# A two-block network in one emission-scheduled kernel: new TensorE estimates in the planner and an explicit wait in the norm

## The chip, the cores and the metric

The kernel runs on one core of a Trainium2 chip. The metric is the device time of one launch in microseconds. It is the median of three runs, which lay within 0.4 us of each other, and one more execution was profiled. Times inside the program (starts, waits, durations) are those of that profiled execution.

## What is computed

The input is 512 tokens of width 1024 in f32. Two blocks of two layers each run one after the other. Cut to what matters, with the first block's token mixers and the loop around them:

```python
def _token_mixers(h, ...):
    a_val, a_gate, q_att, k_att, v_att, q_rec, z_fwd, z_bwd, i_rec, g_rec = split(h @ w_in)
    a = depthwise_conv(a_val * sigmoid(a_gate), conv_w, conv_b)         # 31 taps, 256 channels
    a = silu(layernorm(a))
    att = mixture_of_dilated_attention(q_att, k_att, v_att)             # 6 heads, 3 dilations
    o_r = hgrn2_scan(forward) + hgrn2_scan(backward)                    # 6 heads, gated linear scan
    rec = rmsnorm_per_head(o_r) * rec_norm_w * silu(g_rec)
    return concatenate([a, att, rec]) @ w_out

def first_block(x, ...):
    for l in range(2):
        h = rmsnorm(x) * (1 + sc1) + sh1
        x = x + g1 * _token_mixers(h, ...)
        h = rmsnorm(x) * (1 + sc2) + sh2
        x = x + g2 * ((gelu(conv3(h @ w_up)[gate]) * conv3(h @ w_up)[val]) @ w_down)
    return rmsnorm(x)
```

The second block's layers project in the same way to three attentions (one that keeps the 128 best keys of each query, one over a sliding window with sinks, one of stick-breaking form), mix them with gates and add the result to x.

## The kernel before

**Tiling.** x lies transposed in SBUF, as eight tiles of 128 channels by 512 tokens. A projection is a row of *slots*: a slot is one 128-column piece of a weight matrix times the whole input, that is eight steps over k (`k_step`), each of three matmuls, because a f32 product is made of two rounded halves: high by high, low by high, high by low (`hh,hi`, `hl,hi`, `hh,lo` in the rows). A slot so has 24 matmuls of 128x512, accumulates in one of two PSUM banks called `proj`, and ends with its `consume`, which empties the bank on ScalarE (ACT) or VectorE (DVE). The weights are split into halves on those two engines (`hi<-raw` mostly on ACT, `lo<-raw,hi` on DVE), and an accumulation over the modulation's weights (`ada`) runs on DVE.

**Streams and the planner.** All else, the attentions, the scan, the convolution's norm, the top-k, is written as Python generators, *streams*. While the program is built, the class `Kernel` keeps an estimated clock of TensorE (`self.clock`) and of the other engines (`self.t`), with a cost for each instruction: `charge` for DVE and ACT, `pe` for TensorE. After each `k_step`, `products` lets up to four stream steps (NPUMP) be emitted, of those whose estimated due time has come (`pump`). So the estimates set no instruction and no wait: they decide only between which slot matmuls a stream's instructions stand. Each engine then runs its instructions strictly in that order, and waits by semaphores for what it reads. `bank` lets a stream take a `tr` or `sc` bank of PSUM (two of each) once its readers are estimated to be done.

**The convolution.** Its 31 taps for two channel tiles are 62 multiply-adds on DVE (`conv_taps`). They are emitted where DVE is estimated to be idle for over 0.6 us (FILL, in `charge`), and as a slow stream where DVE's estimated backlog is under 1 us. When all taps are out, the stream `conv_norm` follows: transposes of four into a bank, statistics and scaling on DVE, a square root and a sigmoid on ACT (each needs its own table load), transposes back.

**The order of block 1's mixer.** `block1_layer` lists the slots as `r0 a t0 t1 r1 r2 t2 g P`: scan pair 0, the convolution's inputs, attention pairs 0 and 1, and so on, the scan's three gates (`g`), and then the first half of the output projection (`P`). In layer 0 these are slots 0 to 27 for the inputs and 28 to 31 for `P`. The first of `P` multiplies what the convolution and attention pairs 0 and 1 have left in `mx`, and so has a step ahead of it: `drain("conv","conv","att0","att1")` emits stream steps, of whichever streams are due, until none of those three is alive. While it runs, no slot's matmul is emitted.

**Turn-overs.** Between passes that depend on a norm, the last slots of a pass (the tail) run in halves of 256 tokens, `half_norm` makes the new normalised tiles `hh` and `hl` for each half, and the slots behind wait for those tiles. Weight halves of some tail slots are kept in `hh` and `hl` themselves (`in_h`), until these slots' matmuls are through.

The rows below name PSUM and SBUF tiles: `proj`, `tr`, `sc`, `pva`, `pvs` are banks, `arena` and `stay` are working buffers, `mx` holds mixer outputs, `sm` small statistics, `colt` per-channel constants. A wrapper issues all DVE and ACT work, so that its line is always L113. L346 is the matmul in `mm`, L350 the transpose in `tp`.

Of the kernel before, what the change touches and what calls it, by code (L numbers as in the profile page):

```python
# [116 lines left out]
class Slot:  # L117


    def __init__(self, src, nk, rhs, consume=None, start=True, stop=True, pre=None, name="", parts=None):  # L120
        self.name = name
        self.ada, self.tail = 0, 0
        self.own, self.lead, self.place = None, False, None
# [69 lines left out]
class Kernel:  # L193
# [4 lines left out]
    def __init__(self, ctx, tc, ins, out, cfg):  # L198
# [15 lines left out]
        self.clock = 0.0  # L214
        self.streams = []
# [123 lines left out]
    def pe(self, out, reads, cost):  # L339
        start, rk, wk = self.begin("P", reads, [out])  # L340
        start = max(start, self.clock)
        self.clock = start + cost
        self.end("P", self.clock, rk, wk)

    def mm(self, out, lhsT, rhs, start, stop, cost):
        self.nc.tensor.matmul(out, lhsT, rhs, start=start, stop=stop)  # L346
        self.pe(out, (lhsT, rhs), cost)

    def tp(self, out, in_):
        self.nc.tensor.transpose(out, in_, self.ident)  # L350
        self.pe(out, (in_,), 0.122)
# [188 lines left out]
    def start_up(self):  # L540
# [7 lines left out]
        for _ in range(WARM):  # L548
            self.mm(warm, self.sq2[:, 0:P], self.sq2, True, True, 1.6)
# [46 lines left out]
        for n in range(KT):  # L596
# [16 lines left out]
            for j, (d, p) in enumerate(zip(duo, accs)):  # L613
                self.mm(p, d.raw[:, n * P:(n + 1) * P], self.hraw[n].ap, n == 0, n == KT - 1, 0.858)
# [194 lines left out]
    def k_step(self, s, p, kt, start, stop, c=ALL):  # L809
# [3 lines left out]
        cost = 0.216 if c == ALL else 0.109  # L813
        self.mm(p[:, c], wh, hh, start, False, cost)
        self.mm(p[:, c], wh, hl, False, False, cost)
        self.mm(p[:, c], wl, hh, False, stop, cost)
# [52 lines left out]
    def turn_over(self, i, k):  # L869
# [11 lines left out]
        self.made = [0, 0]  # L881
        for s in tail:
# [75 lines left out]
    def bias_mm(self, bb, duo, kt, only=None):  # L958

        for j, d in enumerate(duo):  # L960
            if only in (None, d):
                self.mm(bb[:, j:j + 1], d.raw[:, kt * P:(kt + 1) * P], self.nB[:, kt:kt + 1], j == 0 and kt == 0,
                        j == len(duo) - 1 and kt == KT - 1, 0.214)
# [86 lines left out]
    def norm_stream(self):  # L1050
# [3 lines left out]
        if st is None:  # L1054
# [3 lines left out]
            for q, sq in enumerate((self.sq, self.sq2)[:1 + fin]):  # L1058
                for j in range(4):
                    self.mm(st[:, 4 * q + j:4 * q + j + 1], sq[:, j * P:(j + 1) * P], self.ones[:, 0:1], True, True, 0.22)  # L1060
# [16 lines left out]
        for b in bufs:  # L1077
            rb = yield from self.bank("tr")
            for j in range(4):
                self.mm(rb[:, j * P:(j + 1) * P], b.ap[:, j * P:(j + 1) * P], self.ident, True, True, 0.226)  # L1080
# [3 lines left out]
    def half_norm(self, hf, c, outs, me, after):  # L1084
# [5 lines left out]
        for q, sq in enumerate(sqs):  # L1090
            for j in range(2):
                self.mm(st[:, 2 * q + j:2 * q + j + 1], sq[:, j * P:(j + 1) * P], self.ones[:, 0:1], True, True, 0.22)
# [13 lines left out]
        for b in bufs:  # L1106
# [3 lines left out]
            for j in range(2):  # L1110
                self.mm(rb[:, j * P:(j + 1) * P], b[:, j * P:(j + 1) * P], self.ident, True, True, 0.226)
# [10 lines left out]
        for n in range(KT + 1):  # L1122
            if n < KT:
                t = self.tmps[n % 2].ap[:, c]
# [43 lines left out]
    def two(self, outs, lhsT, rhs, start, stop, n, k0=0):  # L1168

        for hh in range(2):  # L1170
            self.mm(outs[hh], lhsT[hh], rhs[hh], start, stop, 0.06 if hh == 0 else max(0.858 * n / S, 0.06))

    def pv_add(self, pv, V, j, o, n, rhs, start, stop):

        self.two([pv[64 * h:64 * h + 64, o:o + n] for h in range(2)], [V[:, j, 64 * h:64 * h + 64] for h in range(2)],
                 rhs, start, stop, n)

    def attend(self, heads, span, stride, size, score, V, vo, tag, done, extra=0):
# [9 lines left out]
        for qt in range(5):  # L1188
            if qt < 4:
# [7 lines left out]
                for hh in range(2):  # L1197
                    rows = slice(64 * hh, 64 * hh + 64)
                    self.mm(scs[hh][:, 0:n], q.ap[rows, qt * P:(qt + 1) * P], k.ap[rows, kt0 * P:kt0 * P + n],
                            True, not extra, 0.858 * n / S)  # L1200
# [31 lines left out]
        for kt in (0, 2, 1, 3):  # L1232
# [3 lines left out]
                     [x[:, a:a + n] for x in pts], kt == 0, kt == 3, n)  # L1236
# [104 lines left out]
    def scan_stream(self, l, p, q, T0b, Kb, vbox, gbox, out):  # L1341
# [12 lines left out]
        def scores(w, lhsT, rhs, cost):  # L1354
# [3 lines left out]
            for j in range(4):  # L1358
                for b in range(P // w):
                    k0 = j * P + b * w  # L1360
                    for hh, rows in enumerate(heads):
                        self.mm(scs[hh][b * w:b * w + w, j * w:j * w + w], lhsT[rows, k0:k0 + w], rhs(j, b)[rows],
                                True, True, cost)
# [5 lines left out]
        scs = yield from scores(32, ks.ap, lambda j, b: q.ap[:, j * P + 32 * b:j * P + 32 * b + 32], 0.036)  # L1369
# [9 lines left out]
        for lev in range(7):  # L1379
# [20 lines left out]
            scs = yield from scores(w, km.ap, rhs, 0.036 if w == 32 else 0.083)  # L1400
# [37 lines left out]
        for d in range(2):  # L1438
            for e in range(3):
                i, j = 3 * d + e, 3 - e if d else e  # L1440
                for hh in range(2):
                    self.mm(kv[64 * hh:64 * hh + 64, i * 64:i * 64 + 64],
                            ktb.ap[:, d * S + e * P + 64 * hh:d * S + e * P + 64 * hh + 64],
                            V[:, j, 64 * hh:64 * hh + 64], True, True, 0.083)
# [16 lines left out]
        for e in range(3):  # L1461
            for d in range(2):
                i, j = 3 * d + e, 2 - e if d else e + 1
                c = slice((1 - d) * S + j * P, (1 - d) * S + (j + 1) * P)
                for hh, rows in enumerate(heads):
                    self.mm(pv[rows, j * P:(j + 1) * P], st[rows, i * 64:i * 64 + 64], Q[rows, c], False, e == 2 and d == 1, 0.136)
# [10 lines left out]
        for j in range(4):  # L1477
            self.mm(st[:, 2 * j:2 * j + 2], sq.ap[:, j * P:(j + 1) * P], self.bones, True, True, 0.22)
# [5 lines left out]
        for j in range(4):  # L1484
            self.mm(rb[:, j * P:(j + 1) * P], sq.ap[:, j * P:(j + 1) * P], self.ident, True, True, 0.226)
# [838 lines left out]
```

## Time and profile before

| | us |
|---|---|
| median of 3 runs | 2585.87 (2585.79 to 2586.15) |
| the profiled execution's own time | 2588.26 |
| its span | 2586.5 |
| TensorE busy in the span | 2538.2 (98%), 15404 matmul passes |
| DVE busy | 1773.5 (69%) |
| ACT busy | 1339.2 (52%) |

The profiled execution is 2.39 us above the median, and 1.76 us of its time lie outside the span. To read it: the page's first part tells how little TensorE idles, the waits tell for whom, the windows tell where the other engines are full and where TensorE's clock was lowered, and the timeline of each engine shows the single places.

### The profile page before, as it was taken

How to read it: one execution, taken by the hardware profiler on the slowest of the kernel's cores; microseconds unless marked ns; L12 is line 12 of the kernel's file. 1: busy time of each engine (PE TensorE's matmuls, PEld its weight loads, DVE VectorE, ACT ScalarE, POOL GpSimd, SP SyncE). 2: the span in 40 equal slices, each digit the busy share in tenths (PEclk: the TensorE clock that was granted, in tenths of full speed). 3: DMA queues.
4: the chain of work that ended last, by engine and by line, in shares of the span. 5: the costliest groups of instructions: out<-in, count | busy, mean ns of one | idle time of the engine just before them, and what ended most of it. 6: DMA issues, size and time to landing. Idle time of an engine off the chain costs nothing.

```text
span 2586.5 us, 39181 instructions
## 1 busy us (share of the span) xinstructions
PE 2538.2 (98%) x15404; PEld 1995.5 (77%) x15404; DVE 1773.5 (69%) x3368; ACT 1339.2 (52%) x2345; POOL 0.2 (0%) x4
## 2 busy tenths in 40 slices
PE   9999999999999999999999999999999999999998
PEld 5767788888977768888897677777779667777787
DVE  7897687655689767665667896556556697546645
ACT  4686554323457664442345446666435455666622
POOL 0000000000000000000000000000000000000000
PEclk9999999999999999999999999999999999999999
DMA  7433324444333222443442222223342112222222
GB/s 260 138 136 118 123 99 154 147 147 150 111 137 112 90 106 82 139 141 136 131 139 82 74 77 99 102 94 104 109 129 95 58 70 78 90 78 90 86 90 90
DMA packets 90071, 290.32 MB, mean 112 GB/s; under 512 B 10016, under 2 KB 13728, under 8 KB 89888
## 3 DMA queue, kind: packets, MB, share of 16 engines
q1 hardware_dynamic: 87728, 281.76, 32.1%
q10 hardware_dynamic: 2160, 6.06, 0.7%
q8 instruction: 122, 2.00, 0.3%
q14 instruction: 61, 0.50, 0.1%
HBM read 285.69 MB, written 2.10 MB: 111 GB/s over the span
## 4 chain that ended last, share of the span: by engine, by line
PE 82%; DVE 10%; ACT 4%; DMA 2%; issue 1%; SPq 0%; ACTq 0%; DVEq 0%
PE proj L346 68%; PE sc L346 7%; DVE arena L113 6%; PE tr L350 3%; PE pva L346 3%; ACT arena L113 3%; DVE lo L113 1%; PE pvs L346 1%; ACT L113 1%; DVE sm L113 1%; PE tr L346 1%; DVE hl L113 1%; DVE ada L113 0%; ACT hi L113 0%; DMA arena<-w_in 0%
## 5 line engine op out<-in xcount | busy, mean ns | idle before, releaser
L346 PE MATMUL proj<-hh,hi 128*128 128x512 f32 (+1 forms) x2232 | 896.9, 402 | 7.0 <-DVE arena L113 2.6
L346 PE MATMUL proj<-hl,hi 128*128 128x512 f32 (+1 forms) x2232 | 869.7, 390 | 5.3 <-DVE hl L113 5.3
L346 PE MATMUL proj<-hh,lo 128*128 128x512 f32 (+1 forms) x2232 | 869.8, 390 | 0.5 <-DVE lo L113 0.5
L346 PEld LDWEIGHTS proj<-hh,hi 128*128 128x128 f32 x2232 | 420.2, 188 | 138.3 <-issue 43.9
L113 DVE TENSOR_TENSOR lo<-raw,hi 128x1024 fp32r<-128x1024 f32 (+2 forms) x381 | 436.0, 1144 | 99.4 <-ACT hi L113 95.6
L346 PEld LDWEIGHTS proj<-hh,lo 128*128 128x128 f32 x2232 | 419.9, 188 | 90.3 <-DVE lo L113 1.0
L346 PEld LDWEIGHTS proj<-hl,hi 128*128 128x128 f32 x2232 | 420.7, 188 | 85.4 <-DVE hl L113 8.5
L113 ACT CAST hi<-raw 128x1024 fp32r<-128x1024 f32 (+2 forms) x340 | 333.7, 982 | 100.8 <-PE proj L346 63.6
L346 PE MATMUL proj<-rar,hi 128*128 128x512 f32 x672 | 208.9, 392 | 0.0
L113 DVE SCALAR_TENSOR_TENSOR arena<-proj,colt,arena 128x511 f32<-128x511 f32 x164 | 122.9, 749 | 103.8 <-ACT arena L113 100.9
L113 DVE TENSOR_TENSOR arena<-arena 128x512 f32<-128x512 f32 (+8 forms) x321 | 173.0, 558 | 25.7 <-ACT arena L113 18.8
L113 ACT ACT_TABLE_LOAD x134 | 171.9, 1283 | 17.7 <-DVE sm L113 8.6
L113 ACT COPY arena<-tr 128x512 f32<-128x512 f32 (+3 forms) x266 | 111.2, 458 | 115.3 <-PE tr L350 105.2
L113 DVE SCALAR_TENSOR_TENSOR ada<-ada,cbc 128x1024 f32<-128x1024 f32 x128 | 155.8, 1217 | 0.2 <-DMA ada<-ada 0.2
L346 PEld LDWEIGHTS proj<-rar,hi 128*128 128x128 f32 x672 | 124.9, 188 | 29.7 <-issue 4.6
L346 PE MATMUL sc<-arena 64*32 64x32 f32 (+6 forms) x3024 | 143.8, 248 | 3.5 <-issue 3.1
L113 ACT ACTIVATE arena<-proj 128x512 f32<-128x512 f32 x113 | 66.8, 599 | 155.1 <-PE proj L346 147.4
L113 ACT ACTIVATE arena<-proj,colt 128x512 f32<-128x512 f32 x82 | 56.4, 687 | 170.7 <-PE proj L346 168.5
L346 PE MATMUL proj<-mx,hi 128*128 128x512 f32 x432 | 136.3, 397 | 2.5 <-DVE x L113 2.5
L113 ACT ACTIVATE arena<-arena,sm 128x512 f32<-128x512 f32 (+3 forms) x180 | 105.1, 585 | 59.8 <-DVE sm L113 58.9
L113 DVE SCALAR_TENSOR_TENSOR x<-proj,mod,x 128x512 f32<-128x512 f32 (+1 forms) x102 | 64.6, 634 | 103.8 <-PE proj L346 102.9
L346 PE MATMUL proj<-rar,lo 128*128 128x512 f32 x336 | 130.9, 390 | 0.0
(219 smaller groups left out, 3082.4 us busy)
## 6 DMA issues: line engine op xcount, KB each, us to landing
raw<-w_in SPq DMA_DIRECT2D x190, 512.0 KB, 3.3
ada<-ada SPq DMA_DIRECT2D x128, 512.0 KB, 4.6
raw<-w_up SPq DMA_DIRECT2D x88, 512.0 KB, 3.3
raw<-w_out SPq DMA_DIRECT2D x32, 512.0 KB, 3.4
raw<-w_down SPq DMA_DIRECT2D x32, 512.0 KB, 3.6
raw<-w_br SPq DMA_DIRECT2D x48, 256.0 KB, 2.6
arena<-ada SPq DMA_DIRECT2D x16, 512.0 KB, 7.3
raw<-w_down SPq DMA_DIRECT2D x16, 384.0 KB, 3.2
```

The source lines that it names most:

```text
L113: return f(*a, **kw)
L346: self.nc.tensor.matmul(out, lhsT, rhs, start=start, stop=stop)
L350: self.nc.tensor.transpose(out, in_, self.ident)
```

## The change

Only numbers that set the order change, and one wait in the planning of `half_norm`. The instructions are the same ones.

- `pe` and `mm` no longer take a cost from the caller. `mm` works it out from type, split of the array and width: a 128x512 slot matmul goes from 0.216 to 0.2272 us and a 256-wide one from 0.109 to 0.1205; a pair of 64-row score matmuls (two heads) from 1.716 to 0.877 us; a 32x32 matmul of the scan from 0.036 to 0.022; a transpose from 0.122 to 0.109.
- `self.mode` remembers the split of the array that the last matmul used. A matmul with another split is charged 0.1 us more when it leaves the full array and 0.2 us more otherwise.
- The four warm-up matmuls of each block add 0.74 us each to the clock, beside their new cost.
- `half_norm` now waits, in the planner, while a tile that it is about to write still holds the weight halves of a tail slot whose matmuls are not all emitted (`s.hi is not None`).

```diff
-    def pe(self, out, reads, cost):
+    def pe(self, out, reads, cost, mode):
         start, rk, wk = self.begin("P", reads, [out])
         start = max(start, self.clock)
+        if mode != self.mode:
+            cost += 0.1 if self.mode == (128, 128) else 0.2
+            self.mode = mode
         self.clock = start + cost
         self.end("P", self.clock, rk, wk)

-    def mm(self, out, lhsT, rhs, start, stop, cost):
+    def mm(self, out, lhsT, rhs, start, stop):
         self.nc.tensor.matmul(out, lhsT, rhs, start=start, stop=stop)
-        self.pe(out, (lhsT, rhs), cost)
+        rows, cols, n = lhsT.ap[0][1], lhsT.free_size(), rhs.free_size()
+        mode = tuple(32 if x <= 32 else 64 if x <= 64 else 128 for x in (rows, cols))
+        if lhsT.dtype == F32R:
+            cost = 0.0137 + n * 0.000417
+        elif lhsT.dtype == BF16:
+            cost = 0.0137 + max(n, 64) * 0.000417
+        elif mode == (128, 128):
+            cost = 0.015 + max(n, 128) * 0.00167
+        elif n <= 32:
+            cost = 0.022
+        else:
+            cost = 0.01 + n * 0.000837
+        self.pe(out, (lhsT, rhs), cost, mode)

     def tp(self, out, in_):
         self.nc.tensor.transpose(out, in_, self.ident)
-        self.pe(out, (in_,), 0.122)
+        self.pe(out, (in_,), 0.109, (128, 128))
...
-        cost = 0.216 if c == ALL else 0.109
-        self.mm(p[:, c], wh, hh, start, False, cost)
+        self.mm(p[:, c], wh, hh, start, False)
...
+        self.in_tail = tail
         for s in tail:
...
         for n in range(KT + 1):
             if n < KT:
+                while any(n in s.h_tiles and s.hi is not None for s in self.in_tail):
+                    yield (self.clock + 0.1,)
                 t = self.tmps[n % 2].ap[:, c]
```

**The place between the last gate and the output projection, block 1, layer 0, TensorE.** Before, the end of slot 27 (`proj_2664`) and the first of `P` (`proj_2776<-mx`), with the scan's `pvs`, the attention's `tr` and `sc` between them:

```order
L346 MATMUL proj_2664<-hh,hi_2403 128x512
L346 MATMUL proj_2664<-hl,hi_2403 128x512
L346 MATMUL proj_2664<-hh,lo_2404 128x512
L346 MATMUL proj_2776<-mx,hi_2535 128x512 x2
L346 MATMUL proj_2776<-mx,lo_2536 128x512
L350 MATMUL tr_2780<-ident,arena_89 128x128 x4
L350 MATMUL tr_2786<-ident,arena_89 128x128 x4
L346 MATMUL pvs_2754<-arena_89 64x128 x12
L346 MATMUL sc_2806<-arena_89 128x512
L346 MATMUL sc_2807<-arena_89 128x512
L346 MATMUL proj_2776<-mx,hi_2535 128x512 x2
L346 MATMUL proj_2776<-mx,lo_2536 128x512
```

Now the same place begins with the last matmul of slot 27 (`proj_2676`):

```order
L352 MATMUL proj_2676<-hh,lo_2427 128x512
L368 MATMUL tr_2743<-ident,arena_89 128x128 x4
L368 MATMUL tr_2751<-ident,arena_89 128x128 x4
L352 MATMUL sc_2757<-arena_89 128x512
L352 MATMUL sc_2758<-arena_89 128x512
L352 MATMUL tr_2765<-ident,arena_89 128x128 x4
L368 MATMUL tr_2777<-ident,arena_89 128x128 x4
L368 MATMUL tr_2783<-ident,arena_89 128x128 x4
L368 MATMUL tr_2789<-ident,arena_89 128x128 x4
L352 MATMUL sc_2795<-arena_89 128x512
L352 MATMUL sc_2796<-arena_89 128x512
L368 MATMUL tr_2826<-ident,arena_89 128x128 x4
```

Five more groups of four transposes and the eight rows of `pva` follow before the first matmul on `mx`: the drain stood inside the slots' matmuls before, with `P` running between its parts, and stands now as one piece of 60 stream matmuls and transposes with nothing of a slot in it. Of these, 44 belong to attention pair 2, 12 to the convolution's norm and 4 to the scan.

**The same place on ACT, now.** The rows are part of what the drain emits: the attention's softmax (`arena,sm`), copies out of `tr`, the table loads, and the convolution's square root (`sm_2819<-sm_2806,eps`) and first sigmoid (`arena<-tr_2841,colt`):

```order
L113 COPY stay<-tr_2789 128x4x128
L113 ACTIVATE arena_89,sm_2608<-arena_89,sm_2607 128x512 x2
L113 ACTIVATE arena_89<-arena_89,sm_2608 128x512
L113 ACT_TABLE_LOAD
L113 ACTIVATE sm_2819<-sm_2806,eps 128x4
L113 COPY arena_89<-tr_2826 128x4x128
L113 COPY stay<-tr_2832 128x4x128
L113 ACTIVATE arena_89<-arena_89,sm_2608 128x512
L113 ACT_TABLE_LOAD
L113 ACTIVATE arena_89<-tr_2841,colt 128x512 x2
L113 CAST mx<-arena_89 128x512
L113 COPY arena_89<-tr_2851 128x4x128
```

Before, the convolution's two sigmoids and both its `CAST mx` stood on ACT ahead of the evacuations of the last two gates. Now they stand inside the drain: the second `CAST mx` is the third row below those shown.

**Layer 1, the convolution's norm and the scan of pair 1, TensorE.** Before, four transposes of the convolution (`tr_8161`) stood directly ahead of a scan level's 32 score matmuls (`sc_8171`, `sc_8172`, of which the first two stand here) and its transposes:

```order
L350 MATMUL tr_8161<-ident,arena_5966 128x128 x4
L346 MATMUL sc_8171<-stay,arena_5966 64x64
L346 MATMUL sc_8172<-stay,arena_5966 64x64
...
L350 MATMUL tr_8198<-ident,arena_5966 128x128 x3
L350 MATMUL tr_8203<-ident,arena_5966 128x128 x3
L346 MATMUL proj_8217<-hh,hi_7891 128x512
```

Now slot matmuls stand there, on both sides of the same scan level:

```order
L352 MATMUL proj_8135<-hh,lo_7695 128x512
L352 MATMUL sc_8155<-stay,arena_5960 64x64
L352 MATMUL sc_8156<-stay,arena_5960 64x64
...
L368 MATMUL tr_8182<-ident,arena_5960 128x128 x3
L368 MATMUL tr_8187<-ident,arena_5960 128x128 x3
L352 MATMUL proj_8135<-hh,hi_7694 128x512
```

The convolution's four transposes moved away from these of the scan, to behind the scan's last level and the first of its output matmuls.

## Rows read from the trace of the kernel before

**Rows 1.** Page, busy time, share of span and instructions of each engine.

```profile
PE 2538.2 (98%) x15404; PEld 1995.5 (77%) x15404; DVE 1773.5 (69%) x3368; ACT 1339.2 (52%) x2345; POOL 0.2 (0%) x4
```

**Rows 2.** TensorE's waits by releaser: us in total, times, longest us.

```profile
PE tr L350 <- DVE arena L113: 9.7, 12, 1.1
PE proj L346 <- DVE x L113: 5.4, 8, 1.4
...
PE sc L346 <- issue: 3.1, 4, 1.2
PE tr L350 <- ACT arena L113: 2.9, 3, 1.6
PE proj L346 <- DVE arena L113: 2.6, 2, 2.3
```

**Rows 3.** Windows: length, busy (instructions) of PE, PEld, DVE, ACT, POOL; granted clock, DMA.

```profile
100.00:150.00 50.00, 49.58 (x377) 35.03 (x375) 47.97 (x93) 35.49 (x69) 0.00 (x0) 1.00 0.40 141
...
350.00:400.00 50.00, 50.00 (x222) 41.41 (x221) 37.92 (x50) 21.59 (x31) 0.00 (x0) 1.00 0.46 155
...
885.00:890.00 5.00, 3.37 (x11) 2.67 (x10) 3.98 (x8) 4.16 (x9) 0.00 (x0) 0.66 0.45 156
...
1450.00:1500.00 50.00, 46.59 (x241) 34.04 (x243) 47.91 (x105) 23.82 (x51) 0.00 (x0) 1.00 0.22 74
```

**Rows 4.** PE timeline, slot 18: start, length, what, count, [idle before, releaser].

```profile
162.01 0.50 PE L346 MATMUL proj<-hh,hi 128*128 128x512 f32 x1 [2.30 <-DVE arena L113]
...
164.47 2.08 PE L346 MATMUL sc<-arena,stay 64*128 64x512 f32 x4
166.47 0.50 PE L346 MATMUL proj<-hh,hi 128*128 128x512 f32 x1
...
173.50 1.13 PE L346 MATMUL sc<-arena,stay 64*128 64x512 f32 x4
174.56 0.50 PE L346 MATMUL proj<-hh,hi 128*128 128x512 f32 x1
```

**Rows 5.** DVE timeline ahead of that wait, where block 1's attention and taps meet.

```profile
156.10 0.68 DVE L113 CUSTOM_DVE_ANT_0 arena<-sc,arena 128x512 f32<-128x512 f32 x1
...
158.84 0.49 DVE L113 TENSOR_SCALAR arena<-arena,sm 128x512 f32<-128x512 f32 x1
159.24 2.73 DVE L113 SCALAR_TENSOR_TENSOR arena<-arena,colt 128x512 f32<-128x512 f32 x4
```

**Rows 6.** ACT timeline of the same stretch.

```profile
156.83 0.72 ACT L113 ACTIVATE arena<-arena,sm 128x512 f32<-128x512 f32 x1 [0.60 <-DVE sm L113]
157.46 0.18 ACT L113 ACTIVATION_READ_ACCUMULATOR arena<-arena,sm 128x1 f32 x1
...
158.84 0.72 ACT L113 ACTIVATE arena<-arena,sm 128x512 f32<-128x512 f32 x1
159.58 1.28 ACT L113 ACT_TABLE_LOAD   x1
160.88 1.08 ACT L113 ACTIVATE arena<-proj 128x512 f32<-128x512 f32 x2
```

**Rows 7.** PE timeline in layer 0: transposes, and the eight rows of an attention's `pva`.

```profile
271.89 0.60 PE L350 MATMUL tr<-ident,arena 128*128 128x128 f32 x4
272.24 0.71 PE L346 MATMUL proj<-mx,hi 128*128 128x512 f32 x2
...
289.28 0.64 PE L346 MATMUL pva<-arena 128*64 128x512 f32 x1
...
292.87 0.73 PE L346 MATMUL proj<-mx,hi 128*128 128x512 f32 x2
```

**Rows 8.** DVE timeline in layer 1, the convolution's norm.

```profile
879.58 1.40 DVE L113 BATCH_NORM_STATS2 sm<-arena 128x6 f32<-128x256 f32 x4
...
882.21 1.38 DVE L113 TENSOR_SCALAR arena<-arena,sm,sm 128x256 f32<-128x256 f32 x4
...
886.83 0.69 DVE L113 TENSOR_TENSOR arena<-arena 128x512 f32<-128x512 f32 x1 [0.34 <-ACT arena L113]
```

**Rows 9.** ACT timeline of the same norm.

```profile
884.05 1.28 ACT L113 ACT_TABLE_LOAD   x1 [1.58 <-PE tr L350]
885.35 1.45 ACT L113 ACTIVATE arena<-tr,colt 128x512 f32<-128x512 f32 x2
```

**Rows 10.** PE timeline beside it: the scan's transposes.

```profile
886.85 0.90 PE L350 MATMUL tr<-ident,arena 128*128 128x128 f32 x3 [1.64 <-ACT arena L113]
```

More of the change, by code (lines that the diff above doesn't have):

```diff
@@ L122, in __init__ @@
         self.ada, self.tail = 0, 0
+        self.h_tiles, self.hi = (), None
         self.own, self.lead, self.place = None, False, None
@@ L548, in start_up @@
         for _ in range(WARM):
-            self.mm(warm, self.sq2[:, 0:P], self.sq2, True, True, 1.6)
+            self.mm(warm, self.sq2[:, 0:P], self.sq2, True, True)
+            self.clock += 0.74
         head = 64 if b == 0 else NCOLS
@@ L962, in bias_mm @@
                 self.mm(bb[:, j:j + 1], d.raw[:, kt * P:(kt + 1) * P], self.nB[:, kt:kt + 1], j == 0 and kt == 0,
-                        j == len(duo) - 1 and kt == KT - 1, 0.214)
+                        j == len(duo) - 1 and kt == KT - 1)
     def scaled(self, accs):
@@ L1166, in v_tokens, with two @@
         box.append(j)
-    def two(self, outs, lhsT, rhs, start, stop, n, k0=0):
+    def two(self, outs, lhsT, rhs, start, stop):
         for hh in range(2):
-            self.mm(outs[hh], lhsT[hh], rhs[hh], start, stop, 0.06 if hh == 0 else max(0.858 * n / S, 0.06))
+            self.mm(outs[hh], lhsT[hh], rhs[hh], start, stop)
     def pv_add(self, pv, V, j, o, n, rhs, start, stop):
         self.two([pv[64 * h:64 * h + 64, o:o + n] for h in range(2)], [V[:, j, 64 * h:64 * h + 64] for h in range(2)],
-                 rhs, start, stop, n)
+                 rhs, start, stop)
     def attend(self, heads, span, stride, size, score, V, vo, tag, done, extra=0):
@@ L1199, in attend @@
                     self.mm(scs[hh][:, 0:n], q.ap[rows, qt * P:(qt + 1) * P], k.ap[rows, kt0 * P:kt0 * P + n],
-                            True, not extra, 0.858 * n / S)
+                            True, not extra)
                 self.did = 0.0
@@ L1235, in attend @@
             self.two([pv[64 * h:64 * h + 64, o:o + n] for h in range(2)], [V[:, kt, v:v + 64] for v in vo],
[L1236 removed]
+                     [x[:, a:a + n] for x in pts], kt == 0, kt == 3)
         for x in ptb:
@@ L1352, in scan_stream, with scores @@
         heads = [slice(64 * hh, 64 * hh + 64) for hh in range(2)]
-        def scores(w, lhsT, rhs, cost):
+        def scores(w, lhsT, rhs):
             scs = yield from self.banks("sc")
@@ L1368, in scan_stream @@
         sc32 = scb.ap[:, 0:256].rearrange("p (h n) -> p h n", h=2)
-        scs = yield from scores(32, ks.ap, lambda j, b: q.ap[:, j * P + 32 * b:j * P + 32 * b + 32], 0.036)
+        scs = yield from scores(32, ks.ap, lambda j, b: q.ap[:, j * P + 32 * b:j * P + 32 * b + 32])
         for hh in range(2):
@@ L1399, in scan_stream @@
                 Sin = Sb.ap.rearrange("p (h a b) -> p h a b", h=2, a=4)
-            scs = yield from scores(w, km.ap, rhs, 0.036 if w == 32 else 0.083)
+            scs = yield from scores(w, km.ap, rhs)
             for hh, sc in enumerate(scs):
@@ L1465, in scan_stream @@
                 for hh, rows in enumerate(heads):
-                    self.mm(pv[rows, j * P:(j + 1) * P], st[rows, i * 64:i * 64 + 64], Q[rows, c], False, e == 2 and d == 1, 0.136)
+                    self.mm(pv[rows, j * P:(j + 1) * P], st[rows, i * 64:i * 64 + 64], Q[rows, c], False, e == 2 and d == 1)
         stb.free()
@@ L2172, in in_h @@
             s.place = lambda s, r=slice(2 * j, 2 * j + 2): place(s, r)
+            s.h_tiles = range(2 * j, 2 * j + 2)
     def next_of(self, b, l):
```

28 lines of the change are left out of this document (14 added, 14 removed).

## The prediction

> **What bounds the kernel now.** The page's first part comes first: TensorE is busy 2538.2 of 2586.5 us [rows 1], so all that an order of emission can win is the remaining 48 us, and what it can lose is open. No other engine is full on the mean, DVE with 69% the nearest. The waits say for whom TensorE idles: mostly DVE, in small pieces (12 waits, 9.7 us, none over 1.1), and a few long ones [rows 2]. Some waits at starts and turn-overs are in both orders. The windows show why: there are stretches in which DVE is full, 47.97 of 50 us at 100 to 150 and 47.91 at 1450 to 1500, beside stretches such as 350 to 400 in which TensorE never stops [rows 3]. There it did 222 matmuls in 50.00 us, 0.225 each: the new estimate of 0.2272 fits and the old one of 0.216 was low. A long wait costs more than itself. After the 2.30 us at 162.01 the same four score passes took 2.00 us from start to next start, and later 1.06 [rows 4]; around the wait at 886.85 the granted clock over 5 us is 0.66 [rows 3], so part of it ran at 1.2 instead of 2.4 GHz.
>
> **The change, part by part.**
>
> *The instructions.* None comes or goes: TensorE's work stays the same, and the number of changes of the array's split hardly moves (455 before and 459 after, counted in the two orders). Only waits can change. The new estimates are nearer to the rows (a pair of scores is now 0.877 plus 0.3 for two changes, the row 1.06, the old estimate 1.716), so the planner's clock, which ran behind in the slots and ahead in scores and scans, now shifts work both ways. The DVE and ACT prices stay too low against the rows: the multiply-add is priced at 0.66 us, and four took 2.73 [rows 5].
>
> *The drain ahead of the output projection, block 1, layer 0: +18.* This is the largest term. Before, the convolution's norm was over when slot 28 came, and attention 2 went on between the projection's matmuls. Now the convolution ends late, the drain waits for it, and 60 stream passes stand between slot 27 and slot 28 with no slot matmul. I follow them by hand from the end of slot 27, with prices from rows. Four transposes take 0.35 and, with what the split costs beside them, 0.44 [rows 7]; a score pair 1.06 [rows 4]; one reduction of scores 0.68 and a scaling 0.49 [rows 5]; an exp with its read 0.90, a scaling on ACT 0.72, a table load 1.28, an evacuation 0.54 [rows 6]; a sigmoid with its companion 1.45 [rows 9]; statistics 1.40, normalisation 1.38, a product 0.69 [rows 8].
> Attention 2's first round on ACT: two groups of transposes, copy, load, evacuation of the gate, copy, load, two exps, a cast and a scaling reach 7.7 us (0.44 + 0.54 + 1.28 + 0.54 + 0.54 + 1.28 + 1.80 + 0.54 + 0.72). Its transposes and the next score pair need that scaling: 0.44 and 1.06 make 9.2; two reductions 10.7; the second exp 11.7; DVE scales, then does the convolution's statistics, 14.1 with its small steps; ACT's square root, already loaded, 14.4; normalisation 15.9; ACT's scaling of the last round 16.8, its load 18.1, sigmoid pair 19.5, cast and two copies 21.8 (with the product that the cast waits for). The `pva` rows need the last copy and took 3.59 us in the trace, 292.87 less 289.28 [rows 7]: 25.4 us. TensorE's own work in this is 12 groups of transposes (5.3), two score pairs (2.1) and `pva` (3.6), 11.0. So 14.4 us are idle. After such gaps the rows show half the clock [rows 3, 4]; `pva` is on the chain and would then take 3.6 more. Together +18. Bounds: ACT alone has 18.7 us ahead of `pva` if nothing waits, so 22.3 less 11.0, +11, at the least; with every hand-over 0.2 us dearer and the first matmuls of slot 28 at half clock, +23.
>
> The Trainium skill, page "ScalarE: Activation LUTs", section "What ACT_TABLE_LOAD costs", speaks for a dearer drain: about 1.28 us for the load and as much again, 1.38, for draining the engine, 2.66 for each switch. Against that stands the load at 159.58, behind which the next instruction began 1.30 us later [rows 6], so the trace agrees with the load and not with the second part; by the page the four loads of the chain would add an estimated 5.5 and the sum would be that much later.
>
> *The stalls ahead of it, layer 0: -5.* Slot 18 at 162.01 waited because its bank was emptied late: DVE came late to the scores (156.10), so ACT's exps, its load (159.58) and the evacuations (160.88) were late too [rows 5, 6]. Laying the durations of DVE's rows along both orders, DVE stands about 6 us further ahead from slot 16 to 26 now, since the convolution's taps come out later; locally the attention's scores moved closer to the end of slot 16, which takes back about 2. The 2.30 us and 0.94 for the scores plus 0.7 for the transposes at half clock go for the most part [rows 4], and smaller waits behind DVE at 113 to 274 shrink, of which 1.1 us is the longest [rows 2]: together -3 to -6, I take -5. These are the same taps that are late at the drain.
>
> *Layer 1: -4.5.* At 886.85 a scan's transposes waited 1.64 us [rows 10], because the bank's reader was the convolution's sigmoid behind a table load, 884.05 to 886.8 [rows 9]. Now the convolution's transposes stand elsewhere. That gives back 1.6 and, by the window's 0.66 over 3.37 busy us [rows 3], about 1.5 of clock; two waits of the same kind some 20 and 50 us later probably go (0.9 to 1.1 each, about the longest of the first kind in [rows 2]). The scan's output has less room in the new order. Between -1 and -5.
>
> *The rest: -1.* The top-k stretches, where DVE is full (1450 to 1500 [rows 3]), keep their load; a slightly tighter order costs 0 to 1. Waits in the sliding-window part lose about 1, and the splits' changes come out at -1 to +1. The explicit wait of `half_norm` binds in the planner at two tiles of the feed-forward turn-overs, each by about six half matmuls; what waits behind it on ACT and DVE are the later tiles of the norm, and who needs them is the group's step kt = 6, some 54 half matmuls behind. At half of 0.225 [rows 3] these are 6 us against 0.7: 0, and at most 0.7 for each if that cover were gone.
>
> **The sum.** 18 - 5 - 4.5 - 1 = +7.5 us against the profiled execution's 2588.26, that is 2595.8. It lies 2.39 above the median of 2585.87, and the forecast on that scale is 2593.4, rounded 2593. A measurement of this kernel tells 0.2%, 5.2 us, from no change: under 2580.7 is faster, over 2591.0 slower.
>
> **The rivals.**
>
> *Same.* The drain costs its lower bound of 11 and the two gains come as forecast: 11 - 5 - 4.5 - 1 is about 0, 2586. For it: ACT has room in layer 0 (busy 35.49 of 50 us at 100 to 150 [rows 3]), so copies and loads may lie between the steps that I put behind one another. Against it: nearly all of its rows in the drain follow a TensorE or DVE step of the same chain.
>
> *Faster.* The better estimates take away most waits, not only those I found: the transposes behind DVE (9.7), behind ACT (2.9), slots behind `arena` (2.6) and behind `x` (5.4), and scores behind issue (3.1) [rows 2], together 23.7. The drain at 14.4 without a fall of the clock would leave -9.3, 2576.6. The point from which it decides: the gains must pass the drain by 5.2, so 16 at the least against its lower bound of 11, twice what I found. Against it, DVE's prices, which cause most of those waits, are unchanged.
>
> *Dearer drain.* If a load of another table holds ACT twice as long as its row, which no row shows, the four loads of the chain add 4 x 1.28, 5.1: 2598 to 2599. The Trainium skill's page named above has the rule. A fall of the clock over the whole drain comes to the same.
>
> *The change does nothing here.* If the drain's chain were done by the time slot 27 ends, because DVE and ACT stand further ahead, the three terms vanish in turn; this is part of the case "same". The orders speak against it, since 60 passes lie between the slots.
>
> **How the numbers follow.** Forecast (slower, 2591 to 2597) 0.45; same 0.28; faster 0.16; dearer drain 0.11. Slower is 0.56, same 0.28 and faster 0.16. For 8 in 10 the range runs from 2578, which leaves out the better half of the faster case, to 2602, the drain at +23 with gains of 7: 2585.87 + 16.
>
> **What would show it right or wrong.** In the profile of the changed kernel a stretch of some 25 us at about 265 to 290 us in which TensorE is under half busy, ACT nearly full, the granted clock lowered, and the first matmul on `mx` behind `pva`. The wait of 2.30 at slot 18 and that of 1.64 on the scan's transposes should be gone or under 0.8. Idle of TensorE over the span should rise from 48 to about 53, the rest being lost clock. Wrong would be: the stretch is under 18 us long (chain overlapped), or the waits behind DVE fall by over 10 us in all, or new waits of over 1 us stand in the feed-forward turn-overs, where the norm's explicit wait would be the cause.

## The result: slower by 0.8%, outside the range

The changed kernel takes 2607.07 us (median of four runs, 2604.44 to 2607.45) against 2586.01: ratio 1.0077, 95% interval 1.0064 to 1.0089. The direction was forecast, 2593 was not: the time lies 5 us above the range's upper end. The profiled execution took 2604.44 us, which is the fastest of the four; its span is 16.1 us longer than that of the kernel before.

The page's first part and TensorE's longest groups of waits after the change (us in total, times, longest us):

```profile
PE 2543.9 (98%) x15404; PEld 1995.3 (77%) x15404; DVE 1773.2 (68%) x3368; ACT 1340.2 (51%) x2346; POOL 0.2 (0%) x4
```

```profile
PE tr L368 <- DVE arena L113: 19.3, 20, 4.5
PE proj L352 <- DVE hl L113: 6.1, 8, 1.7
PE proj L352 <- ACT arena L113: 4.8, 5, 1.6
PE tr L368 <- ACT arena L113: 3.4, 4, 1.9
PE proj L352 <- DVE x L113: 2.2, 6, 0.4
```

The time that TensorE is not busy rose from 48.3 to 58.7 us, where I had forecast 53. Against [rows 1, 2]: the other engines do the same work, TensorE waits 10 us more for transposes that read what DVE writes, with one wait of 4.5. Slot matmuls that wait for ACT rose from 1.7 us in 3 waits to 4.8 in 5, while those behind `x` fell from 5.4 to 2.2. TensorE's busy time is 5.7 us longer at the same 15404 passes. The lower clock is a part of that, 1.6 us at the most: TensorE is busy for 16.9 us at a granted clock of 0.50 in the trace before and for 20.0 in this one. The rest was not traced.

The drain ahead of slot 28 stands where it was forecast. TensorE's timeline from slot 27's last matmuls to slot 28's first, and the windows over it (columns as in [rows 3]):

```profile
259.95 1.21 PE L368 MATMUL tr<-ident,arena 128*128 128x128 f32 x8
...
268.77 1.94 PE L368 MATMUL tr<-ident,arena 128*128 128x128 f32 x8 [4.50 <-DVE arena L113]
270.64 2.08 PE L352 MATMUL sc<-arena 64*128 64x512 f32 x4
274.80 1.98 PE L368 MATMUL tr<-ident,arena 128*128 128x128 f32 x8 [2.09 <-DVE arena L113]
278.02 1.35 PE L368 MATMUL tr<-ident,arena 128*128 128x128 f32 x4 [1.25 <-DVE arena L113]
...
282.55 1.11 PE L368 MATMUL tr<-ident,arena 128*128 128x128 f32 x4 [1.87 <-ACT arena L113]
...
286.37 1.06 PE L352 MATMUL pva<-arena 128*64 128x512 f32 x1
...
287.22 0.68 PE L352 MATMUL pva<-arena 128*64 128x512 f32 x1
...
289.98 0.73 PE L352 MATMUL proj<-mx,hi 128*128 128x512 f32 x2
```

```profile
265.00:270.00 5.00, 1.23 (x6) 1.26 (x7) 2.87 (x7) 3.31 (x8) 0.00 (x0) 0.69 0.30 115
270.00:275.00 5.00, 2.91 (x9) 1.04 (x8) 2.22 (x8) 2.59 (x7) 0.00 (x0) 0.50 0.00 0
275.00:280.00 5.00, 3.54 (x14) 2.37 (x14) 3.37 (x14) 4.12 (x7) 0.00 (x0) 0.50 0.01 3
280.00:285.00 5.00, 2.38 (x11) 1.58 (x10) 1.39 (x2) 4.08 (x6) 0.00 (x0) 0.50 0.00 0
285.00:290.00 5.00, 5.00 (x20) 1.47 (x18) 1.38 (x2) 2.06 (x3) 0.00 (x0) 0.76 0.00 0
```

From 259.95 to 289.98 are 30.0 us without a slot matmul, with TensorE busy 1.23 to 3.54 of 5 us in the middle and at half clock for most of it. No engine is full there: ACT, which I had forecast nearly full, is busy 2.59 to 4.12 of each 5 us. It is a chain that goes from one to the next, as ACT shows:

```profile
273.48 0.72 ACT L113 ACTIVATE arena<-arena,sm 128x512 f32<-128x512 f32 x1 [2.15 <-DVE sm L113]
...
275.63 1.28 ACT L113 ACT_TABLE_LOAD   x1
276.92 0.30 ACT L113 ACTIVATE sm<-sm,eps 128x4 f32<-128x4 f32 x1
...
279.75 1.28 ACT L113 ACT_TABLE_LOAD   x1
281.05 1.45 ACT L113 ACTIVATE arena<-tr,colt 128x512 f32<-128x512 f32 x2
283.26 0.62 ACT L113 CAST mx<-arena 128x512 fp32r<-128x512 f32 x1 [0.76 <-DVE arena L113]
```

Each load again took 1.28 us, and the next instruction began 1.29 to 1.30 after the load's start, as in [rows 6].

**Where all the time went.** In the two traces I took, for each pair of neighbouring matmul passes, the time from start to start, less the median of the same kind of pair in the trace before, and summed it by the slot in which it lies. What is left over is waits and time at the lower clock. The kind of a pair is given by the shapes of its two passes and by whether they are passes of one instruction. The first row is that sum in us for the kernel before, the others the difference to it, from one profiled execution each:

| | 0-26 mixer, layer 0 | 27-35 output projection | 36-103 feed-forward | 104-139 mixer, layer 1 | 208-289 block 2, layer 0 | 290-332 layer 1, top-k part | 333-389 rest of layer 1 | whole program |
|---|---|---|---|---|---|---|---|---|
| before | 34.9 | 7.5 | -0.3 | 28.5 | 26.8 | 18.9 | 8.4 | 128.5 |
| after | -3.3 | +15.3 | +0.3 | -3.5 | +1.7 | +0.8 | +4.3 | +15.6 |
| e1 conv early | -5.2 | +9.9 | +0.3 | +5.2 | +1.1 | +0.7 | +4.4 | +16.2 |
| e2 drain named | -0.9 | +11.1 | +0.3 | -3.8 | +1.1 | +0.8 | +4.4 | +13.1 |
| e3 new in block 1 | -1.8 | +16.0 | +0.3 | -1.7 | -0.4 | -0.1 | 0.0 | +12.9 |
| e4 new in block 2 | -0.6 | 0.0 | 0.0 | -1.5 | +0.6 | +0.7 | +4.4 | +3.1 |
| e5 no split charge | -7.6 | +22.2 | +0.3 | -2.3 | -1.4 | -2.6 | +6.6 | +15.5 |
| e6 old score price | -4.2 | +4.8 | +0.3 | +0.9 | +7.0 | +6.1 | +2.1 | +17.1 |
| e7 old slot price | -3.7 | +30.2 | 0.0 | -5.2 | -2.3 | -3.5 | +0.2 | +15.7 |
| e8 dearer DVE | -4.1 | +16.3 | 0.0 | +3.7 | -4.4 | -4.9 | -0.2 | +6.1 |
| e9 scores only | -9.7 | +17.6 | 0.0 | +2.8 | -2.7 | -6.2 | +5.1 | +7.2 |
| e10 split charge only | -0.7 | -1.5 | 0.0 | +3.8 | +6.4 | +3.4 | -0.4 | +10.5 |
| e11 scan only | -10.2 | +22.0 | 0.0 | -2.1 | 0.0 | -0.1 | 0.0 | +9.8 |
| e12 composed | +2.2 | -0.1 | +0.2 | -2.2 | -4.1 | -4.9 | -0.2 | -9.0 |

Regions with the same order in two kernels tell what one execution's scatter is. In slots 0 to 26, after, e2 and e3 have one order and range from -3.3 to -0.9, and before, e4 and e12 have one order and range from -0.6 to +2.2. In slots 104 to 139, after, e2, e3 and e12 range from -3.8 to -1.7. In slots 333 to 389, after, e1, e2 and e4 agree within 0.1. So a difference of 2 or 3 us in slots 0 to 26 or 104 to 139 of a single trace tells little. Some pairs of an order have no like in the trace before; how these are counted moves a cell by up to 3 us (the most in e7, slots 27 to 35).

**The second loss** is the sliding-window part of block 2's layer 1 (+4.3), where I expected a gain. ACT's timeline there, and the slot that waits:

```profile
2452.66 1.28 ACT L113 ACT_TABLE_LOAD   x1
2453.95 0.51 ACT L113 ACTIVATE arena<-arena,sm 128x256 f32<-128x256 f32 x1
...
2455.16 1.28 ACT L113 ACT_TABLE_LOAD   x1
2456.45 0.60 ACT L113 ACTIVATE arena<-proj 128x512 f32<-128x512 f32 x1
```

```profile
2457.10 0.50 PE L352 MATMUL proj<-hh,hi 128*128 128x512 f32 x1 [1.59 <-ACT arena L113]
```

The attention's exps stand on ACT ahead of the evacuation of a slot's bank, with a table load on either side, and the slot after the next one waits for that bank. In the order before, 3 to 9 of the slot's own matmuls stood behind such a step; after, several steps stand directly behind a slot's last matmul, ahead of its evacuation. In the trace before, at the like place:

```profile
2449.35 0.51 ACT L113 ACTIVATE arena<-arena,sm 128x256 f32<-128x256 f32 x1 [0.73 <-DVE sm L113]
...
2450.56 1.28 ACT L113 ACT_TABLE_LOAD   x1
2451.85 0.60 ACT L113 ACTIVATE arena<-proj 128x512 f32<-128x512 f32 x1
```

There the evacuation began 1.8 us after the start of its slot's last matmul, at 2450.01; after the change 4.2 us, 2456.45 against 2452.21. Four waits of this kind (0.41, 0.81, 1.59 and 0.73) make 3.5 of the 4.3. The other orders bear this out, though none was built to move these steps alone: before, e3, e7, e8, e11 and e12 have no such step in slots 333 to 389 and no slot matmul there waits over 0.25 us for ACT; after, e1, e2 and e4 have six each and wait 3.5 to 3.6 us. e5, e6 and e9 have two or three and wait 3.5, 1.0 and 3.9 us; e10 has one and no such wait.

### The profile page after: what moved, and what is told of

The parts are those of the page before. It is cut to its first block, busy times and chain, and to the rows that moved or that the text cites. A ratio compares the mean times of both kernels' runs of the same rounds, so it can differ in the third digit from the quotient of the medians.

```text
span 2602.6 us, 39230 instructions
## 1 busy us (share of the span) xinstructions
PE 2543.9 (98%) x15404; PEld 1995.3 (77%) x15404; DVE 1773.2 (68%) x3368; ACT 1340.2 (51%) x2346; POOL 0.2 (0%) x4
## 4 chain that ended last, share of the span: by engine, by line
PE 86%; DVE 8%; ACT 3%; DMA 1%; issue 1%; SPq 0%; ACTq 0%; DVEq 0%
PE proj L352 71%; PE sc L352 7%; DVE arena L113 5%; PE tr L368 3%; PE pva L352 3%; ACT arena L113 2%; PE pvs L352 1%; DVE sm L113 1%; DVE lo L113 1%; PE tr L352 1%; DVE hl L113 1%; ACT L113 1%; DMA arena<-w_in 0%; DMA raw<-w_in 0%; DMA colt<-cols 0%
## 5 line engine op out<-in xcount | busy, mean ns | idle before, releaser
L352 PEld LDWEIGHTS proj<-hl,hi 128*128 128x128 f32 x2232 | 420.2, 188 | 89.2 <-DVE hl L113 10.5
L113 ACT CAST hi<-raw 128x1024 fp32r<-128x1024 f32 (+1 forms) x341 | 334.0, 981 | 111.3 <-PE proj L352 70.9
L113 DVE TENSOR_TENSOR arena<-arena 128x512 f32<-128x512 f32 (+9 forms) x335 | 177.1, 551 | 28.7 <-ACT arena L113 21.2
L113 ACT COPY arena<-tr 128x512 f32<-128x512 f32 (+3 forms) x270 | 112.3, 454 | 117.9 <-PE tr L368 108.3
L352 PE MATMUL sc<-arena 64*32 64x32 f32 (+6 forms) x3032 | 154.4, 253 | 2.2 <-issue 0.9
L368 PE MATMUL tr<-ident,arena 128*128 128x128 f32 x786 | 123.6, 282 | 26.7 <-DVE arena L113 19.3
L113 ACT ACTIVATE arena<-proj 128x512 f32<-128x512 f32 x123 | 72.9, 599 | 148.2 <-PE proj L352 134.4
L113 ACT ACTIVATE arena<-arena,sm 128x512 f32<-128x512 f32 (+3 forms) x193 | 112.9, 585 | 62.5 <-DVE sm L113 60.6
L368 PEld LDWEIGHTS tr<-ident,arena 128*128 128x128 f32 x786 | 95.0, 144 | 61.7 <-ACT arena L113 19.7
```

The source lines that it names most:

```text
L113: return f(*a, **kw)
```

## The experiments

The first four take the change apart by place, the next four by its estimates, then three single estimates and one version composed of the regions. `mm` and `pe` are those of the change. In the diffs of e3, e4 and e9 to e12, the kernel before is the base, with the norm's wait added.

**e1, the convolution earlier.**

```diff
-                    self.spawn(conv(), "conv", True)
+                    self.spawn(conv(), "conv")
```

> The changed kernel with one edit: the convolution's taps are no longer a slow stream, so they come out earlier and the drain ahead of slot 28 finds the convolution done. Block 2 keeps the order of the changed kernel, instruction for instruction. Theory 1 (the drain alone is the loss of block 1): the piece of 60 passes is gone, 16 us come back, about 2591 us. Rival 2 (the late taps were what made the earlier slots quicker, so undoing them brings the old waits behind DVE back): only 10 to 12 us come back, 2595 to 2597. If the drain's idle time was taken from later slots anyway, nothing comes back: 2605.

Measured 2606.04, ratio 1.0075 (1.0063 to 1.0088): nothing came back, which is the third of the three outcomes expected. The piece was gone, slot 28 followed slot 27 at once, but slot matmuls waited in its place: 3.65 us for `x` at slot 29, and 4.29 in layer 1, where the same edit brought a wait that the changed kernel did not have.

```profile
269.17 0.73 PE L352 MATMUL proj<-mx,hi 128*128 128x512 f32 x2 [3.65 <-DVE x L113]
...
931.01 1.22 PE L352 MATMUL proj<-mx,hi 128*128 128x512 f32 x2 [4.29 <-DVE arena L113]
```

So the drain of 15.3 was exchanged for 9.9 at the output projection and 8.7 more in layer 1. Rival 2 had the right thought, that taps which come earlier put others behind, but neither the size nor the place: slots 0 to 26, where it looked for the old waits, were no worse than after the change (-5.2 against -3.3). That the earlier taps took DVE's time from what is waited for here is likely, and not shown.

**e2, a drain that emits only what it waits for.** The same order up to slot 27.

```diff
-            if not self.pump():
+            if not self.pump(live if names[:1] == ("conv",) else None):
```

> The changed kernel, same order up to the drain, but the drain ahead of the output projection emits only the streams it waits for: 16 passes (12 of the convolution, 4 of attention 2) in place of 60. It tells what sets the drain's length. Theory 1a (attention 2's softmax stands in the way on ACT and DVE): the stretch from slot 27 to slot 28 falls from 27 to about 13 us, the time by 7 to 9, to 2599. Rival 1b (the convolution's own chain of norm, square root and sigmoids sets it): the stretch stays over 20 us, the time within 3 us of 2607.

Measured 2600.47, ratio 1.0051 (1.0037 to 1.0065): 6.6 us less than the changed kernel. The stretch fell from 30.0 to 12.2 us, but the loss in slots 27 to 35 only from 15.3 to 11.1, since the convolution's chain is still waited for: 5.37 us at its transposes, and 3.40 at the first slot matmul, for `mx`. Theory 1a holds for the length: attention 2 made more than half of it. It was not the whole price. By the table, from one execution each, only 2.5 us separate the two kernels, because the changed kernel's profiled execution lies 2.6 below its median and this one 1.2 above.

**e3 and e4, the new estimates in one block only.**

```diff
+    def new(self):
+        return getattr(self, "cur", -1) < 208     # e3; >= 208 in e4
...
+        if self.new():
+            if lhsT.dtype == F32R:
+                cost = 0.0137 + n * 0.000417
...
-        self.pe(out, (in_,), 0.122)
+        self.pe(out, (in_,), 0.109 if self.new() else 0.122, (128, 128))
```

> New estimates and the norm's wait while block 1 is emitted, the old estimates in block 2: the order of block 1 is that of the changed kernel, the attentions of block 2 have that of the kernel before. Theory 1 (block 1: drain +16.5, other waits -7; block 2: new waits +6.5): 2586 + 9.5, about 2595.5. Rival 3 (block 2 gives nothing, the whole loss is in block 1): 2605 to 2607.

> The other half: old estimates in block 1 with the norm's wait (82 positions of 18075 differ there from the kernel before, all in layer 0's feed-forward), new estimates in block 2. Theory 1: block 2 costs 6.5 us by new waits, most of them in layer 1's sliding-window part, about 2592.5. Rival 3: 2586 to 2587. The norm's wait itself is expected to cost nothing.

Measured 2598.59 (ratio 1.0048, 1.0036 to 1.0061) and 2592.82 (1.0025, 1.0016 to 1.0035). Rival 3 falls: e4 came out as theory 1 said, e3 3 us above it. Against the 2586.32 of these runs the halves cost 12.3 and 6.5, together 18.8 of the 21 that the change costs. e4 also holds the norm's wait with nothing else changed in block 1, and the feed-forward of slots 36 to 103 lost 0.0: the wait costs nothing there.

**e5 to e7, one estimate back to the old one.** In this order: the charge for the split, the price of 64-row scores, the price of the slots.

```diff
-            cost += 0.1 if self.mode == (128, 128) else 0.2
```

> The changed kernel without the charge for a change of the array's split; all other new estimates stay. In its order the drain ahead of slot 28 is gone, and in layer 1 of block 2 the sliding window's exps stand at the slots' ends as in the kernel before. Theory 4 (the charge is what delays the convolution and shifts the exps): drain 0 and the new waits of block 2 mostly gone, about 2584 to 2589. Rival 5 (with the first experiment in mind: without the drain the waits come back at the output projection's own matmuls, whatever the estimate): 2595 to 2606.

```diff
-            cost = 0.01 + n * 0.000837
+            cost = 0.858 * n / S if mode == (64, 128) else 0.01 + n * 0.000837
```

> The changed kernel with the old price of the 64-row score matmuls (0.858 us each at 512 wide, in place of 0.4385); the charge for changes of the split stays. Its order has no drain ahead of slot 28 either. Theory 4 (charge alone): block 2's new waits of about 5 us stay in its layer 1, block 1 is without the drain, about 2592. Theory 6 (the scores' price is what matters, since a cheaper score puts its exps and reductions closer to the slots that follow): block 2 loses its waits as well, 2584 to 2588.

```diff
-            cost = 0.0137 + n * 0.000417
+            cost = 0.216 if n == 512 else 0.109
         elif lhsT.dtype == BF16:
```

> The changed kernel with the old price of the slot matmuls (0.216 and 0.109 us). Its order has a longer drain ahead of slot 28: 105 stream passes in place of 60, 43 of them the scan's. Theory 1 (a drain costs what its chain of DVE and ACT takes beyond TensorE's own work): the scan's steps lie beside the softmax, so the stretch is longer by 5 to 10 us and the time 2608 to 2615. Rival (the slots' price made the order bad, and the old one is better): below 2600.

Measured 2604.87 (1.0071, 1.0058 to 1.0083), 2605.99 (1.008, 1.0066 to 1.0094) and 2603.96 (1.0067, 1.0055 to 1.008): no one of them alone brings the time back. The places differ, though. What the text on e5 says of its order was an oversight of mine: the drain is there, with 118 passes, 62 of them the scan's, and lost 22.2; and its sliding window, whose waits I expected to be mostly gone, lost 6.6. e7's longer drain lost 30.2, the most of all: there theory 1 had the direction, though the stretch grew from 30.0 to 44.6 us and not by 5 to 10. The kernel won elsewhere, which the expected total left out, and its time fell between the two that were expected. e6 had no drain and lost 4.8 there, and lost 13 in the top-k parts of block 2, which theory 6 did not have at all. Theory 4 falls.

**e8, DVE dearer in the planner.**

```diff
-            c = 0.067 + n * (0.00052 if fast else 0.00104)
+            c = 0.067 + n * (0.00056 if fast else 0.00112)
```

> The changed kernel with the planner's price of VectorE per element raised by 8% (0.00104 to 0.00112 us), nearer to the rows of its trace. No drain ahead of slot 28 in its order. Theory 7 (the TensorE estimates became right, and the too low price of VectorE is what still lets streams run early): waits behind VectorE fall below those of the kernel before, 2575 to 2584. Rival 5 (what the order gains in one place it loses in another): 2588 to 2600.

Measured 2598.93, ratio 1.0053 (1.004 to 1.0065). Here too a drain stood ahead of slot 28, of 94 passes, which I had overlooked for the same reason, and it lost 16.3. Block 2 gained 9.5 us against the kernel before, all of it in the parts ahead of the sliding window, and the sliding window's waits were gone. Theory 7 holds in block 2, rival 5 in block 1 and for the total.

**e9 to e11, one new estimate alone.** The scores, the charge for the split, the scan's matmuls.

```diff
+        if mode == (64, 128) and lhsT.dtype == F32:                 # e9
+            cost = 0.01 + n * 0.000837
...
+        if mode != self.mode:                                       # e10
+            cost += 0.1 if self.mode == (128, 128) else 0.2
+            self.mode = mode
...
+        if mode[0] < 128 and mode[1] < 128:                         # e11
+            cost = 0.022 if n <= 32 else 0.01 + n * 0.000837
```

> The kernel before (and the norm's wait) with one new estimate: the 64-row score matmuls cost 0.4385 us at 512 wide in place of 0.858. In its order the convolution's norm begins at slot 27 in place of 23, and 96 stream passes of attention 2, the scan and the convolution stand ahead of slot 28. Theory 8 (a cheaper price for what lies between the slots lets the planner's clock of TensorE run slower against that of VectorE, so the taps, which wait for VectorE to look idle, come out later): slots 27 to 35 lose 15 to 20 us, the time 2598 to 2606. Rival 9 (only all estimates together do this): within 5 us of 2586.

> The kernel before (and the norm's wait) with one new item: the charge of 0.1 or 0.2 us for each change of the array's split. It makes the clock of TensorE run faster, and in its order the convolution's norm begins at slot 23 as before, with no drain ahead of slot 28. Theory 8: no loss at slots 27 to 35, and the sliding-window part of layer 1 keeps the new waits of 4 to 5 us if the charge is what moves its exps; 2584 to 2592. Rival 9: 2595 or more.

> The kernel before (and the norm's wait) with one new estimate: the scan's small matmuls (0.022 in place of 0.036 us for 32 wide, 0.064 in place of 0.083 for 64). The convolution's norm begins only at slot 28 in its order, and 154 stream passes stand ahead of slot 28, 94 of them the scan's. Theory 8: the longest drain so far, 20 to 30 us lost at slots 27 to 35, 2604 to 2614. Rival (the scan's passes fill the gaps, so a longer piece is no dearer): 2596 to 2602.

Measured 2596.91 (1.0038, 1.0025 to 1.005), 2599.61 (1.0055, 1.0043 to 1.0068) and 2599.36 (1.0049, 1.0037 to 1.0062). At slots 27 to 35 theory 8 is borne out three times: the scores alone lose 17.6, the scan alone 22.0, the charge alone wins 1.5. The first two gain about 10 us in slots 0 to 26, which the expected totals left out: e9 and e11 came in under them. Whether the later taps are what gains there is not shown: after the change they are as late, and the gain is 1 to 3. e11's total lies in the range of its rival, that a longer piece is no dearer; the 22.0 at the place, against 15.3 after the change, speaks against that rival. e10's total is well over the 2584 to 2592 expected, mostly because of block 2. There the charge does not move the sliding window's exps (-0.4), the scores do (+5.1); the charge loses 9.8 in the parts with top-k, where the scores gain 8.9. In the change these two nearly cancel there.

**e12, composed.** Old estimates up to slot 35, new ones after, and DVE's price up by 1/13 from slot 208 on.

```diff
+    def new(self):
+        return getattr(self, "cur", -1) >= 36
...
-            c = 0.067 + n * (0.00052 if fast else 0.00104)
+            up = 14 / 13 if getattr(self, "cur", -1) >= 208 else 1.0
+            c = 0.067 + up * n * (0.00052 if fast else 0.00104)
```

> A version put together from the regions measured so far: the old estimates up to slot 35, the new ones from slot 36 on, and VectorE's price raised by 1/13 in block 2. By its order layer 0's mixer is that of the kernel before, layer 1's mixer that of the changed kernel, and block 2 nearly that of the run with the dearer VectorE. If the regions add up: 2586 - 3.5 (layer 1) - 9.5 (block 2), 2573. If what is won in one region is lost in the next: 2584 or more.

Measured 2576.29, ratio 0.9961 (0.9947 to 0.9975): faster than both kernels, by 10.6 us than the kernel before, and 3 us above the 2573 expected. Block 2 and layer 1 came in as they had been measured in other kernels (block 2: -9.2 here, -9.5 in e8; layer 1's mixer -2.2, and -1.7 to -3.8 in the kernels of the same order). Layer 0's mixer, with the order of the kernel before, shows +2.2, which is scatter. TensorE's waits in it:

```profile
PE proj L353 <- DVE hl L113: 6.3, 8, 1.7
PE proj L353 <- DVE x L113: 3.7, 7, 1.1
PE tr L373 <- DVE arena L113: 3.0, 7, 0.8
```

The transposes behind DVE, 9.7 us in [rows 2] and 19.3 after the change, are down to 3.0.

## Why the prediction was wrong

*The drain, +18: right in mechanism, place and nearly in size.* Slots 27 and 28 hold 18.9 us of waits and lost clock after the change. The kernel before had 1.2 there already, which my term did not take off, and 2.5 come back in slots 29 to 35, so the net is about 15.3. The stretch was 30.0 us, where the chain and its 3.6 of lost clock made 29.0. The first matmul on `mx` stood behind `pva`, as said. Half the clock fell on other steps than I had put it: the second round's eight transposes took 1.87 to the next start and its score pair was 2.08 long, and `pva` took 4.5 instead of 7.2. The rival of dearer table loads is refuted at this place by the rows above: the second part that the Trainium skill, page "ScalarE: Activation LUTs", section "What ACT_TABLE_LOAD costs", adds to each load does not show in them.

*Its cause.* I said that the convolution ends late. The runs with one estimate, and the orders that their kernels emit, show why: cheaper scores and scan matmuls, which lie between slot matmuls, make the planner's clock of TensorE advance less for the same work on DVE; DVE then looks less idle, and the taps, which are emitted only where it looks idle, come later. From slot 8 to slot 22 the planner's clock advances by 126.0 us before, 117.4 with the scores alone, 112.3 with the scan alone, 131.6 with the split charge alone and 121.8 after the change. In the emitted orders the norm of the convolution begins at slot 23 before and with the split charge alone, at 27 with the scores alone and after the change, at 28 with the scan alone.

*The stalls ahead of it, -5: measured -3.3 in this trace, -0.9 and -1.8 in e2 and e3 with the same order: too large.* The part of the -3.3 that lies ahead of slot 4, -1.3, is scatter, since e4, with the order of the kernel before, has -1.1 there. The 2.30 us at slot 18 are gone, as said, and slot 18 gains 4.5. New waits came in their place, here 1.47 us at 119.93 and 0.87 at 130.07; slots 13 and 14 lose 3.8 us together in all three kernels.

*Layer 1, -4.5: measured -3.5* (and -3.8, -1.7 and -2.2 in e2, e3 and e12 with the same order). The wait of 1.64 at the scan's transposes went; one of 1.02 followed at 912.09.

*The rest, -1: measured +7.1. This step failed.* Of the 7.1, 4.3 are the sliding window and 2.5 the rest of block 2; e4, with the new estimates in block 2 alone, is 6.5 us slower than the kernel before. I followed the order of block 2 for the top-k part and the splits, put the sliding window at a gain of 1, and did not look at what stands on ACT between a slot's last matmul and its evacuation. The prices for it were in [rows 6]: a load of 1.28, two exps, a second load. That explains the 4.3 of the sliding window; the 2.5 were not followed to their steps. The norm's wait, inside the same term, was right at 0.

*The scale.* The four terms give 2595.8 for a profiled execution, and 2604.44 was measured: 8.6 short, of which the last term is 8.1, the two gains 2.7 and the drain -2.7. The other 5 us of the miss of 14 come from scatter between executions: I took the profiled execution's 2.39 above the median as an offset to keep, and after the change the profiled one was 2.63 below it. Runs of one kernel mostly span 2 to 5 us here (e6: 2605.29 to 2609.86), so the range needed that width on top.

*Chances.* "Slower" at 0.56 was the right case, though no form of it held the loss in block 2; the rival "same" assumed the drain's lower bound and no loss in block 2. The faster rival named DVE's price as its obstacle: e8 and e12 fit that, since in block 2 the new TensorE estimates lose 6.8 us by the table, and win 9.5 and 9.2 with DVE's price raised too. The drain's lower bound is 11, and the 16 that the faster case needed were not twice the gains I had found but one and a half times the 10.5.

What is still open: why the charge for the split loses 6.4 and 3.4 us in the parts with top-k (e10). Its waits are on transposes behind DVE, 14.3 us in 25 waits, but which emission decision brings them there was not traced.

## What to carry to other kernels

An estimate that is nearer to the truth helps a greedy planner only if its rivals are as near: here correcting one engine's prices changed who looked idle, and a good order that the old prices had given was lost. Look first at the points where the emission must stop for a stream (a drain, an evacuation that frees a bank): here the loss came from a chain of small steps on all engines, not from the busy time of any of them. When an order can be set by region, measure the regions apart and compose them; here that gave 2576 us from pieces of the kernel before and of kernels that were all slower than it.

## What the hardware showed that was not expected

In the drain TensorE ran at 1.2 GHz (granted clock 0.50) for some 20 us on end: the three windows from 270 to 285 show 0.50, and the 0.69 and 0.76 of their neighbours stand for 3.1 and 2.4 us more. In these three it was busy 2.38 to 3.54 of 5 us. The clock came back only within the dense `pva` passes, of which the third pair took 0.68 us and the second 1.06. In the kernel before, the single wait of 2.30 us was followed by some 3.4 us of it, by the same working (columns as in [rows 3]):

```profile
160.00:165.00 5.00, 2.99 (x13) 2.44 (x15) 4.28 (x7) 4.99 (x8) 0.00 (x0) 0.80 0.07 30
165.00:170.00 5.00, 5.00 (x21) 2.94 (x18) 4.96 (x12) 4.46 (x9) 0.00 (x0) 0.86 0.58 206
```

Here, then, a wait of 4.50 us with a chain of waits of 0.21 to 2.09 us behind it held the clock down about six times as long as the one wait of 2.30 us did.
